# Four residual additions per column pair done by accumulating transfers instead of VectorE, in the gate stage of a one-core encoder block

## The chip, the cores and the metric

The kernel runs on one core of one Trainium2 chip. A core has TensorE for matrix products, VectorE and ScalarE for elementwise work, GpSimd (called POOL in the profile) and SyncE (SP), which here only issues transfers. The time is device microseconds of one execution; the runs before the change took 2024.7, 2026.38 and 2027.43 us, median 2026.38. An instruction of the profile carries the line of the kernel that made it, "L420" for line 420; a line can belong to a helper that many places call.

## The reference

One layer of a streaming encoder works on x, 256 rows of 4096 columns, all in f32. Attention and a convolution branch give y, which is projected and added to x. What the change touches comes after that:

```python
h = h + jnp.concatenate([y_a, y_c], axis=-1) @ w_out[i]
gate = jax.nn.sigmoid(rms_norm(h, ple_norm_g[i]) @ w_ple_gate[i] + b_ple_gate[i])
h = h + gate * (p[i] @ w_ple[i])
return rms_norm(h, final_g)
```

So the last stage needs the product of the normalised h with w_ple_gate (4096 x 4096), a bias per column, a sigmoid, a small product p @ w_ple (inner size 256), the gated residual addition, and the sum of squares of the new h per row for the final norm, whose weight is final_g.

## The kernel before, in words

**Products in two parts.** Each f32 matrix is split into a high part (cast to fp32r on ScalarE, L204) and a low part (subtracted on VectorE, L205); a product is the sum of three matmuls, high by high, low by high and high by low. All these matmuls into the large products come from line 420, those of the small embedding product from L237, those of weights kept back for the end of the last pair from L408.

**Column pairs.** The 4096 columns are eight blocks of 512, taken two at a time: four pairs, c0 = 0, 2, 4, 6. The 256 rows are two halves of 128, so a pair has four quarters (half h, block j), in the order (0,0), (1,0), (0,1), (1,1), and four PSUM banks that collect its product. The inner 4096 is cut into 16 units of 256 rows of weights. A plain unit is 24 matmuls. A unit marked * in an order such as `dense` uses a scheme of seven products instead of eight (21 matmuls); for it VectorE forms sums of weight tiles (L518, L519, L531, L532), and four more PSUM banks hold the helper sums P1, P5, P7 and P6. These four come from the same four banks (`ps_tmp`) into which the small product p @ w_ple goes. The order `dense` begins "1 0* 3 2*", so the helper banks are first needed in the second unit of a pair, unit 1 when counted from 0. Orders of the last stage hold eight * units, the order `final` of the last pair seven; its last three units are kept back as parts (`left`) and multiplied at the end quarter by quarter, with line-by-line order fixed by hand.

**Filler work.** Work that may run beside the products is put into a queue, `later`. After each unit `fill(4)` takes four entries from its front and traces them. The end of a pair puts work there that runs during the next pair's units: `gated_pair` (L1236) appends four products "embedding times gate" (which read, and so free, the `ps_tmp` banks) and then, quarter by quarter, the residual addition, the square sum and the weighting by final_g.

**What sets the order.** The program is traced in order, but a planner orders the instructions of each engine before the run. It gives a slot of a tile's buffers when one is free in its own reckoning, and it prefers what was traced first, yet fills an engine with later work whenever the earlier isn't ready by its reckoning. On the chip each engine then runs its list strictly in order and waits where it must. Only instructions under `pin` keep the written order. Weight tiles have five buffers (`wpool`), high parts and low parts three each, rows of bias and of final_g three (`row`). SP issues weight loads at L482 and the rows at L1071 (`broadcast_row`); POOL issues accumulating transfers, which in the stages before add one operand to a tile while they load it (L463, L495, L524). In the gate stage POOL issues none.

**The tail.** After the last pair come the kept-back products, both halves' norms and the stores, all pinned.

Of the kernel before, what the change touches and what calls it, by code (L numbers as in the profile page):

```python
# [13 lines left out]
ALU = mybir.AluOpType  # L14
# [3 lines left out]
NB = 512  # L18
# [7 lines left out]
def hybrid_block(  # L26
# [23 lines left out]
    nc = tc.nc  # L50
# [129 lines left out]
    later = deque()  # L180
# [62 lines left out]
    def product(w, col, lhs, kblocks, pool=None, tag="acc", fills=2):  # L243

        acc = [
            (pool or ps_acc).tile([P, NB], F32, tag=tag, name=f"acc{h}") for h in range(NH)
        ]
        for k0 in range(0, kblocks, KC):
            kc = min(KC, kblocks - k0)
            wh, wl = weight_parts(w, col, k0, kc)  # L250
            for k in range(kc):
                for h in range(NH):
                    accumulate(acc[h], h, lhs, k0 + k, wh, wl, k, kblocks)
            fill(fills)
        return acc
# [121 lines left out]
    def mixed_product(  # L377
# [93 lines left out]
        for n, (pair, seven, by_dma) in enumerate(order):  # L471
# [82 lines left out]
            if begins and on_begin:  # L554
                on_begin()
# [13 lines left out]
    tt, stt = nc.vector.tensor_tensor, nc.vector.scalar_tensor_tensor  # L569
    QUARTERS = ((0, 0), (1, 0), (0, 1), (1, 1))  # L570

    def helper_sums(helper, z):


        nc.scalar.copy(z[1][0], helper["P1"])
        tt(z[1][0], helper["P6"], z[1][0], ALU.add)
        tt(z[0][1], helper["P5"], z[1][0], ALU.add)
        tt(z[1][0], helper["P7"], z[1][0], ALU.add)
        tt(z[1][1], helper["P5"], z[1][0], ALU.add)

    def sum_tiles(*homes):

        homes = homes or (dict(tag="stage"),) * 2
        t = [spool.tile([P, NH, NB], F32, name="z", **kw) for kw in homes]
        return t, [[t[j][:, h] for j in range(2)] for h in range(NH)]
# [57 lines left out]
    def first_pairs(add):  # L643
# [62 lines left out]
        for n in range(1, n_x + 1):  # L706
# [26 lines left out]
    rows = [(conv_ln_g, KCW), (conv_ln_b, KCW), (b_dw, KCW), (attn_out_g, AW // P),  # L733
            (conv_out_g, KCW), (ple_norm_g, KD)]
# [332 lines left out]
    def broadcast_row(src, n0, n, **kw):  # L1067

        kw = kw or dict(tag="row", bufs=3)
        t = spool.tile([P, n], F32, name="row", **kw)  # L1070
        nc.sync.dma_start(  # L1071
            t, bass.AP(tensor=src.tensor, offset=src.offset + n0, ap=[[0, P], [1, n]])
        )
        return t
# [13 lines left out]
    for c0, order in zip(range(0, CW // NB, 2), point):  # L1088
        row = broadcast_row(b_pw, c0 * NB, 2 * NB, tag="stage")
        rows = [row[:, j * NB : (j + 1) * NB] for j in range(2)]  # L1090
# [106 lines left out]
    for c0 in range(0, D // NB, 2):  # L1197
        for j in range(2):
            hc = act.tile([P, NH, NB], F32, tag="act", name="hc")
            c = c0 + j  # L1200
# [19 lines left out]
        for h, j in QUARTERS:  # L1220
            hc = hs[c0 + j][:, h, :]
# [10 lines left out]
    ssq_f = cpool.tile([P, NH, n_f + 2], F32, name="ssq_f")  # L1232
    nc.vector.memset(ssq_f[:, :, :1], EPS)
    square_f = partial(square_sum, scale=D ** -0.5)

    def gated_pair(c0, order, ahead):  # L1236

        z, rows, fgs = [], [], []

        def on_begin():  # L1240
            rows.extend(broadcast_row(b_ple_gate, (c0 + j) * NB, NB) for j in range(2))

        def on_helpers(helper):
            z.extend(sum_tiles()[1])
            stt(z[0][0], helper["P1"], r_h[:, :1], rows[0], ALU.mult, ALU.add)
            helper_sums(helper, z)
            for h, j in QUARTERS[1:]:
                zz = z[h][j]
                stt(
                    zz, zz, r_h[:, h : h + 1], rows[j],  # L1250
                    ALU.mult, ALU.subtract if j else ALU.add,
                )
            fgs.extend(broadcast_row(final_g, (c0 + j) * NB, NB) for j in range(2))

        acc = mixed_product(
            w_ple_gate[0], c0 * NB, hT, hS, order, on_helpers, ahead=ahead, fills=(4,),
            on_begin=on_begin,
        )
        pacc = [
            product(w_ple[0], (c0 + j) * NB, pT, PLE // P, pool=ps_tmp, tag="tmp", fills=0)  # L1260
            for j in range(2)
        ]
        todo = []
        for h, j in QUARTERS:
            gt, hc = z[h][j], hs[c0 + j][:, h, :]
            stt(gt, acc[h][j], r_h[:, h : h + 1], gt, ALU.mult, ALU.subtract if j else ALU.add)
            nc.scalar.activation(gt, gt, AF.Sigmoid)
            later.append(partial(tt, gt, pacc[j][h], gt, ALU.mult))
            todo.append(partial(tt, hc, hc, gt, ALU.add))
            todo.append(partial(square_f, ssq_f[:, h, 1 + c0 + j : 2 + c0 + j], hc))  # L1270
            todo.append(partial(tt, hc, hc, fgs[j], ALU.mult))
        later.extend(todo)

    for c0 in range(0, n_f - 2, 2):
        gated_pair(c0, dense if c0 else late, None if c0 else h_ahead)


    c0 = n_f - 2
# [9 lines left out]
    rows, fgs = [], []  # L1288

    def on_begin():  # L1290
        rows.extend(broadcast_row(b_ple_gate, (c0 + j) * NB, NB) for j in range(2))

    def scaled(h, j):
        zz = z[h][j]
# [2 lines left out]
    def on_helpers(helper):  # L1297
# [3 lines left out]

    acc, add_left = mixed_product(
        w_ple_gate[0], c0 * NB, hT, hS, final, on_helpers, fills=(4,), on_begin=on_begin,
        left=[None] * 3 + [kept] * 3,
    )
# [73 lines left out]
    squares = []  # L1379
# [45 lines left out]
```

## Time and profile before

| | before |
|---|---|
| median of three runs | 2026.38 us |
| profiled execution, its own time | 2025.85 us |
| span of that execution in the trace | 2024.1 us |
| instructions | 26329 |
| granted TensorE clock | 0.998 |
| HBM read | 441.78 MB |

The time outside the span is 2025.85 - 2024.1 = 1.75 us. The gate stage is the last part of the span, from about 1690 us to the end. A busy share is an average over the whole span, and TensorE's includes the overlap of pipelined matmuls: a matmul of 128 x 512 is shown with 391 ns, while one starts about every 227 ns. Lost time of TensorE is therefore read from how many matmuls a stretch holds.

### The profile page before, as it was taken

Reading aid. Unit: us, or ns where it says so; the run is one execution under the profiler, and the core shown is the slowest. Engines: PE = TensorE matmul, PEld = TensorE weight load, DVE = VectorE, ACT = ScalarE, POOL = GpSimd, SP = SyncE. Lnnn points to the kernel's source line nnn. Section 1 sums busy time; section 2 is a strip of 40 time slices with the busy share of each in tenths; the row PEclk is TensorE's granted clock in tenths of the full one; section 3 lists DMA queues with packets and bytes.
Section 4 is the critical chain, followed back from the end, with each engine's and each line's share of the span. In section 5 each row is a group of like instructions: output and inputs, shape, how many; then the busy total and the mean of one; then the engine's idle time right before and its main releaser. Section 6 shows DMA issues by size and latency. Waiting matters only on the chain.

```text
span 2024.1 us, 26329 instructions
## 1 busy us (share of the span) xinstructions
PE 2006.7 (99%) x9043; PEld 1648.0 (81%) x9043; DVE 1926.9 (95%) x2771; ACT 1257.1 (62%) x1634; POOL 65.3 (3%) x71
## 2 busy tenths in 40 slices
PE   9999999999999999999999999999999999999997
PEld 7888888878888888788888888887888888888876
DVE  7999999899999999888999999999999999999998
ACT  7655555665666556776566676765766766656565
POOL 0000000000000000000000000000000000000000
PEclk9999999999999999999999999999999999999999
DMA  8788878679668877556677786876767766666765
GB/s 290 225 233 241 249 221 250 178 220 257 200 198 257 255 206 235 164 176 205 202 239 215 225 244 209 240 239 204 236 215 230 234 200 200 211 218 206 232 207 180
DMA packets 174193, 447.72 MB, mean 221 GB/s; under 512 B 14302, under 2 KB 17518, under 8 KB 174058
## 3 DMA queue, kind: packets, MB, share of 16 engines
q1 hardware_dynamic: 161952, 417.93, 63.8%
q0 software_dynamic: 11456, 27.27, 7.9%
q8 instruction: 71, 1.16, 0.2%
q10 hardware_dynamic: 650, 0.84, 0.1%
q14 instruction: 64, 0.52, 0.1%
HBM read 441.78 MB, written 4.19 MB: 220 GB/s over the span
## 4 chain that ended last, share of the span: by engine, by line
PE 89%; DVE 6%; issue 2%; DMA 1%; ACT 1%; POOLq 0%; POOL 0%; ACTq 0%; DVEq 0%; SPq 0%
PE acc L420 68%; PE acc_P L420 17%; DVE wl L205 2%; DMA wt<-in_w_in_dram 1%; PE tmp_ps L170 1%; DVE cv L787 1%; PE acc L237 1%; DVE ul L205 1%; PE tmp_ps L959 0%; PE tmp_ps L943 0%; PE tmp_ps L977 0%; ACT uh L204 0%; DVE cv L868 0%; ACT wh L204 0%; PE tmp_ps L982 0%
## 5 line engine op out<-in xcount | busy, mean ns | idle before, releaser
L420 PE MATMUL acc<-wh,big_t 128*128 128x512 f32 x4028 | 1240.3, 391 | 0.9 <-ACT big_t L156 0.4
L204 ACT CAST wh<-wt 128x1024 fp32r<-128x1024 f32 (+1 forms) x716 | 684.3, 965 | 493.8 <-PE acc L420 351.7
L420 PEld LDWEIGHTS acc<-wh,big_t 128*128 128x128 f32 x4028 | 753.3, 188 | 157.1 <-issue 1.3
L205 DVE TENSOR_TENSOR wl<-wt,wh 128x1024 fp32r<-128x1024 f32 (+1 forms) x716 | 788.8, 1113 | 33.0 <-ACT wh L204 27.5
L420 PE MATMUL acc<-wl,big_t 128*128 128x512 f32 x1958 | 756.4, 392 | 0.3 <-DVE wl L205 0.2
L420 PEld LDWEIGHTS acc<-wl,big_t 128*128 128x128 f32 x1958 | 367.2, 188 | 78.1 <-DVE wl L205 2.7
L204 ACT CAST uh<-ua 128x1024 fp32r<-128x1024 f32 x187 | 196.6, 1051 | 103.0 <-DVE ua L519 51.7
L205 DVE TENSOR_TENSOR ul<-ua,uh 128x1024 fp32r<-128x1024 f32 x187 | 228.1, 1220 | 6.9 <-ACT uh L204 4.2
L787 DVE SCALAR_TENSOR_TENSOR cv<-uT,dw,cv 128x255 f32<-128x255 f32 (+23 forms) x480 | 203.6, 463 | 1.1
L420 PE MATMUL acc_P<-uh,big_t 128*128 128x512 f32 x570 | 174.6, 391 | 0.1
L204 ACT CAST uh<-ub 128x1024 fp32r<-128x1024 f32 x99 | 104.2, 1053 | 47.9 <-DVE ub L532 39.2
L420 PEld LDWEIGHTS acc_P<-uh,big_t 128*128 128x128 f32 x570 | 106.0, 188 | 24.5 <-ACT uh L204 3.3
L205 DVE TENSOR_TENSOR ul<-ub,uh 128x1024 fp32r<-128x1024 f32 x99 | 120.8, 1220 | 0.8 <-ACT uh L204 0.5
L420 PE MATMUL acc_P<-ul,big_t 128*128 128x512 f32 x285 | 109.7, 392 | 0.2 <-DVE ul L205 0.2
L420 PE MATMUL acc<-uh,big_t 128*128 128x512 f32 x286 | 88.6, 390 | 0.0
L420 PE MATMUL acc_P<-wh,big_t 128*128 128x512 f32 x286 | 88.3, 389 | 0.0
L518 DVE TENSOR_TENSOR ua<-wt 128x512 f32<-128x512 f32 x112 | 76.9, 686 | 10.0 <-DMA wt<-in_w_in_dram 6.2
L519 DVE TENSOR_TENSOR ua<-wt 128x512 f32<-128x512 f32 x112 | 76.8, 686 | 2.7 <-DMA wt<-in_w_in_dram 1.7
L420 PE MATMUL acc_P<-uh,comb_t 128*128 128x512 f32 x228 | 70.3, 391 | 0.3 <-ACT uh L204 0.2
L532 DVE TENSOR_TENSOR ub<-ub,wt 128x512 f32<-128x512 f32 x99 | 68.1, 688 | 1.4
L531 DVE TENSOR_TENSOR ub<-ua,wt 128x512 f32<-128x512 f32 x99 | 67.8, 685 | 0.0
L420 PEld LDWEIGHTS acc_P<-ul,big_t 128*128 128x128 f32 x285 | 53.3, 188 | 13.9 <-DVE ul L205 3.0
(254 smaller groups left out, 1631.0 us busy)
## 6 DMA issues: line engine op xcount, KB each, us to landing
wt<-in_w_in_dram SPq DMA_DIRECT2D x416, 512.0 KB, 4.7
wt<-in_w_out_dram SPq DMA_DIRECT2D x128, 512.0 KB, 4.5
wt<-in_w_ple_gate_dram SPq DMA_DIRECT2D x128, 512.0 KB, 4.2
wt<-in_w_pw_dram SPq DMA_DIRECT2D x32, 512.0 KB, 4.9
ua<-in_w_in_dram SPq DMA_DIRECT2D x31, 512.0 KB, 4.3
ua<-in_w_in_dram POOLq DMA_DIRECT2D x31, 512.0 KB, 8.8
wt<-in_w_in_dram SPq DMA_DIRECT2D x31, 256.0 KB, 2.8
low<-in_w_in_dram POOLq DMA_DIRECT2D x12, 512.0 KB, 8.2
```

Source lines behind the costliest of these rows:

```text
L170: nc.tensor.transpose(pt[:, i * T + h * P : i * T + (h + 1) * P], src[:, h, b] if len(src.shape) == 4 else src[:, h, b * P : (b + 1) * P], ...
L204: nc.scalar.copy(wh[:, :kc, :], wt[:, :kc, :]),
L205: nc.vector.tensor_tensor(wl[:, :kc, :], wt[:, :kc, :], wh[:, :kc, :].bitcast(F32), ALU.subtract),
L237: nc.tensor.matmul(acc, a, b[:, k, :], start=kb == 0 and kind == 0, stop=kb == kblocks - 1 and kind == 2,)
L420: nc.tensor.matmul(banks[name], a, b, start=name not in begun, stop=final and ends[name] == n and kind == 2 and not (left and name in "P2 ...
L518: plus(ua[:, 0], w0[:, 0], w0[:, 1])
L519: plus(ua[:, 1], w0[:, 1], w1[:, 1])
L531: plus(ub[:, 0], ua[:, 0], w1[:, 1])
L532: plus(ub[:, 1], ub[:, 0], w1[:, 0])
L787: nc.vector.scalar_tensor_tensor(cv[:, i, PAD - k :], uT[:, i, : T + k - PAD], dw[:, b, k : k + 1], cv[:, i, PAD - k :], ALU.mult, ALU.add,)
```

## The change

In `gated_pair` the residual addition `hc + gt`, a VectorE instruction on 128 x 512 values, becomes a transfer issued by POOL that adds the tile `gt` onto `hc` in place. The queue `later` is refilled in another order: for each quarter the product, then its transfer (eight entries), then eight empty entries, then the four square sums, then the four weightings. With four entries per unit, the square sums are traced in unit 4 of the next pair and the weightings in unit 5. The products of the last two quarters are traced in unit 1 instead of unit 0. The two loads of a pair's bias rows, issued before in the first unit with helper sums, become two entries at the end of the same queue, in all four pairs. The last pair's own residual additions stay on VectorE.

The change's short name also speaks of seven products in a ninth pair and of three low parts by transfers in two groups; the diff has no line for that, and the kernel before has both already (the order `denser` has nine * units, and three marked "-").

```diff
+    def bias_row(rows, c):
+        rows.append(broadcast_row(b_ple_gate, c * NB, NB))
+
     def gated_pair(c0, order, ahead):
 
         z, rows, fgs = [], [], []
 
         def on_begin():
-            rows.extend(broadcast_row(b_ple_gate, (c0 + j) * NB, NB) for j in range(2))
+            later.extend(partial(bias_row, rows, c0 + j) for j in range(2))
...
-        todo = []
+        squares, weights = [], []
         for h, j in QUARTERS:
             gt, hc = z[h][j], hs[c0 + j][:, h, :]
             stt(gt, acc[h][j], r_h[:, h : h + 1], gt, ALU.mult, ALU.subtract if j else ALU.add)
             nc.scalar.activation(gt, gt, AF.Sigmoid)
             later.append(partial(tt, gt, pacc[j][h], gt, ALU.mult))
-            todo.append(partial(tt, hc, hc, gt, ALU.add))
-            todo.append(partial(square_f, ssq_f[:, h, 1 + c0 + j : 2 + c0 + j], hc))
-            todo.append(partial(tt, hc, hc, fgs[j], ALU.mult))
-        later.extend(todo)
+            later.append(partial(nc.gpsimd.dma_start, hc, gt, accum_op=ALU.add))
+            squares.append(partial(square_f, ssq_f[:, h, 1 + c0 + j : 2 + c0 + j], hc))
+            weights.append(partial(tt, hc, hc, fgs[j], ALU.mult))
+        later.extend([lambda: None] * 8 + squares + weights)
...
     def on_begin():
-        rows.extend(broadcast_row(b_ple_gate, (c0 + j) * NB, NB) for j in range(2))
+        later.extend(partial(bias_row, rows, c0 + j) for j in range(2))
```

## The prediction

> **What bounds it now.** I read the page first, then a table of four stretches of the last stage, then the chain of waits for the edges of its column pairs, and last the timelines of VectorE, ScalarE and TensorE around one edge. From the page:
>
> ```profile
> span 2024.1 us, 26329 instructions
> PE 2006.7 (99%) x9043; PEld 1648.0 (81%) x9043; DVE 1926.9 (95%) x2771; ACT 1257.1 (62%) x1634; POOL 65.3 (3%) x71
> PE 89%; DVE 6%; issue 2%; DMA 1%; ACT 1%; POOLq 0%; POOL 0%; ACTq 0%; DVEq 0%; SPq 0%
> ```
>
> TensorE is the bound, VectorE is nearly as full. Since a busy TensorE is not TensorE at its peak, I price its lost time in the part that the diff can touch: from the first matmuls behind pair 0 to the last of the final pair. The chain of waits, cut to three windows, gives the edges:
>
> ```profile
> 1740.13 5.44 PE acc L237 x24
> ...
> 1827.88 5.44 PE acc L237 x24
> ...
> 1915.73 5.44 PE acc L237 x24
> ```
>
> Twenty-four undisturbed matmuls take 5.44 us, so one takes 0.2267. The table by stretches (span, then busy time and count by engine, granted clock, DMA share, GB/s; the fourth and fifth rows are the L420 and L408 matmuls alone):
>
> ```profile
> 1745.57:1833.32 87.75, 87.70 (x386) 71.56 (x385) 87.02 (x106) 52.42 (x64) 0.00 (x0) 1.00 0.67 217
> 1833.32:1921.17 87.85, 87.85 (x385) 71.64 (x385) 86.98 (x107) 51.92 (x64) 0.00 (x0) 1.00 0.69 215
> 1921.17:1993.08 71.91, 71.73 (x309) 56.45 (x307) 70.82 (x87) 44.06 (x53) 0.00 (x0) 1.00 0.66 208
> ...
> 1921.17:1993.08 71.91, 67.88 (x291) 53.25 (x290) 1.00 0.66 208
> 1921.17:1993.08 71.91, 4.01 (x17) 3.19 (x17) 1.00 0.66 208
> ```
>
> By the code a middle pair has 8 units of 21 matmuls, 8 of 24 and 24 for the embedding: 384, or 87.04 us. It takes 87.75 and 87.85, so 0.71 and 0.81 are lost. In the final pair 291 + 17 = 308 matmuls are 69.81 us of 71.91: 2.10 lost. Together **3.6 us** is all that TensorE loses there. VectorE is idle for 0.73, 0.87 and 1.09 us of the same stretches and ScalarE for some 35 us of a pair: whatever is lost, VectorE is the engine that is late.
>
> **Removed: twelve additions.** Groups by line, last stage:
>
> ```profile
> L184 DVE TENSOR_TENSOR hc<-hc,row 128x512 f32<-128x512 f32 x12 | 8.2, 687 | 0.0
> L184 DVE TENSOR_TENSOR hc<-hc,z 128x512 f32<-128x512 f32 x12 | 8.1, 685 | 0.0
> ```
>
> The second group goes: 4 x 0.685 = 2.74 us of VectorE per pair boundary, three times, 8.2 us. It cannot bring 8.2. TensorE has only 0.71, 0.81 and 2.10 to win in the stretches behind the three boundaries, each less than 2.74. So the gain is between 0 and 3.6. It is 0 if the lost slivers come from hand-overs between ScalarE and VectorE and not from the backlog; it is 3.6 if the backlog is all. Since the high and low parts have three buffers each, VectorE can't keep 2.74 us of lead for 70 us; I take somewhat under half, 1.5.
>
> **Added: twelve transfers on POOL.** Each is 128x512 f32, 256 KB, read twice and written once, all inside SBUF. The trace has no such transfer; the nearest rows are the accumulating loads, and plain ones of that size. Two lines of POOL issues (L495's landing, then L524's issue and landing) and the page's list of issues:
>
> ```profile
> DMA to landing us min/median/max: 5.8/7.0/9.3
> ...
> L524 POOL DMA_DIRECT2D low<-in_w_out_dram x6: 859/860/872, 1445.6 to 1615.2; - x6
> DMA to landing us min/median/max: 8.0/8.7/10.0
> ...
> low<-in_w_out_dram POOLq DMA_DIRECT2D x9, 512.0 KB, 8.4
> ...
> row<-in_b_ple_gate_dram SPq DMA_DIRECT2D x8, 256.0 KB, 4.7
> ...
> out_dram<-hc SPq DMA_DIRECT2D x12, 256.0 KB, 2.4
> ```
>
> Issue: 0.86 us each on POOL, which has 0.00 busy in all three stretches, so it costs nothing; without that cover it would be 12 x 0.86 = 10.3 us. Landing: not under the 2.4 of a plain store from SBUF, not over the 8.7 of an accumulating load of twice the bytes; I take 5.5, between the plain 4.7 and the accumulating 7.0. The Trainium skill's page "DMA: Bandwidth & Descriptors", section "Anatomy of one DMA — SWDGE (gpsimd) path", fits 2.0 us plus bytes over 436e3 per microsecond, an estimate of 2.6 us here; the trace does not agree, for the same fit gives 3.2 us for the 512 KB rows that took 7.0 and 8.7. By the fit the square's wait below would vanish and the sum would be 0.3 us better.
>
> Do they crowd out weights? Three transfers of twice the size fall into one stretch of the output projection:
>
> ```profile
> 1438.83:1460.00 21.17, 21.17 (x93) 17.38 (x93) 20.47 (x27) 15.51 (x18) 2.58 (x3) 1.00 0.97 262
> ```
>
> The DMA share is 0.97 there against 0.67, and 93 matmuls in 21.17 us are 0.2276 each, the full pace within a count. Four transfers of half the size bring less. Cost 0; at worst the 0.2 us that these 93 lie above 0.2267, per boundary.
>
> **Moved: two products.** Transfers now stand between the products, so of the first four entries taken in unit 0 two are transfers, and the products of quarters (0,1) and (1,1) slip into unit 1. They empty two PSUM banks that unit 1's helper sums P7 and P6 need. At the second boundary VectorE, ScalarE and TensorE ran so:
>
> ```profile
> 1832.68 1.88 DVE L184 TENSOR_TENSOR z<-acc,z 128x512 f32<-128x512 f32 x3
> ...
> 1836.28 0.69 DVE L531 TENSOR_TENSOR ub<-ua,wt 128x512 f32<-128x512 f32 x1
> 1836.94 1.23 DVE L205 TENSOR_TENSOR wl<-wt,wh 128x1024 fp32r<-128x1024 f32 x1
> ...
> 1839.82 1.29 DVE L184 TENSOR_TENSOR hc<-hc,z 128x512 f32<-128x512 f32 x2
> 1841.02 1.22 DVE L205 TENSOR_TENSOR wl<-wt,wh 128x1024 fp32r<-128x1024 f32 x1
> 1842.16 1.22 DVE L205 TENSOR_TENSOR ul<-ub,uh 128x1024 fp32r<-128x1024 f32 x1
> ```
> ```profile
> 1835.85 1.06 ACT L204 CAST wh<-wt 128x1024 fp32r<-128x1024 f32 x1 [2.05 <-PE acc L420]
> ...
> 1838.61 2.00 ACT L204 CAST wh<-wt 128x1024 fp32r<-128x1024 f32 x2 [0.76 <-ACT uh L204]
> 1840.52 1.05 ACT L204 CAST uh<-ub 128x1024 fp32r<-128x1024 f32 x1
> 1841.46 0.63 ACT L610 ACTIVATE junk<-hc 128x512 bf16<-128x512 f32 x1
> ```
> ```profile
> 1838.60 0.62 PE L420 MATMUL acc_P<-wh,big_t 128*128 128x512 f32 x2
> ...
> 1839.96 0.62 PE L420 MATMUL acc_P<-uh,big_t 128*128 128x512 f32 x2
> ...
> 1842.00 0.62 PE L420 MATMUL acc_P<-uh,big_t 128*128 128x512 f32 x2
> ```
>
> The slots that unit 1 gives to filler work are those where two additions ran at 1839.82. With two products fewer ahead of them they come 1.2 us sooner (three took 1.88), near 1838.6, or in the gap that opens before the low part at 1836.94, which waits for a cast that TensorE releases. The banks are then free at about 1839.3 and 1839.9; P7 starts at 1839.96 and P6 at 1842.0. It fits, barely: cost 0, at worst the rival below.
>
> **Moved: squares, weightings, bias rows.** Four squares (ScalarE) and four weightings (VectorE, 0.687 us) keep their number and go to units 4 and 5; eight empty entries make the distance. The two bias-row loads are issued behind the weightings instead of in unit 1. Their 0.33 us on SP's queue are the same; they are read some 13 units later, so a landing of 4.7 us is hidden, and their wait for a free row no longer stands ahead of weights by order of the program. Cost 0. But the planner fills idle engines with any ready work. Behind the first pair of the output projection, ScalarE:
>
> ```profile
> 1403.28 0.63 ACT L610 ACTIVATE junk<-hc 128x512 bf16<-128x512 f32 x1 [1.31 <-DVE hc L1222]
> ...
> 1406.55 1.03 ACT L204 CAST wh<-wt 128x1024 fp32r<-128x1024 f32 x1
> 1407.61 1.05 ACT L204 CAST uh<-ua 128x1024 fp32r<-128x1024 f32 x1
> ```
>
> Two of the four squares in this group belong, in program order, behind unit 1's casts of 1406.55 and 1407.61, and ran before them; ScalarE even held 1.31 us for the first. So a square may be put ahead of its transfer's real landing, with unit 1's and 2's casts queued behind it and VectorE's low parts behind these. If kept in unit 4 it has some 15 us, and nothing is late. I charge 0.1 us per boundary, 0.3 in all.
>
> **Sum.** -1.5 + 0.3 = -1.2 us. The profiled execution took 2025.85, its span 2024.1 and 1.75 outside; it becomes 2024.65. The median of the runs shown, 2026.38, lies 0.53 above it, so I forecast **2025.2**.
>
> **Rivals.** *All of the lost time returns*: 2026.38 - 3.6 = 2022.8. For it: VectorE is over 98% busy wherever TensorE loses, and 2.74 exceeds every loss. Against: three buffers cap its lead. *Nothing moves*, 2026.4: the freed time becomes idle VectorE, or a different planned order eats it.
>
> *Squares run ahead*, on the slower side. The transfer of quarter (1,0) goes out after its product, about 1834; at the upper landing, 8.7 us, it is there at 1842.7. If its square sits in ScalarE's hole before 1838.61, the casts behind it wait 4.1 us; 0.76 of that is idle now, and the low parts lie 1.1 us ahead of their matmuls (1841.02 + 1.22 against the end of unit 1's 21, 1838.60 + 4.76). TensorE loses the other 2.2 us; the second two transfers land within the delay. Three boundaries: 6.6 - 1.2 = +5.4, 2031.8. It decides once a transfer lands over 2 us later than the planner believes. For it: the squares at 1403.28. Against: the 35 us of slack of ScalarE and a landing nearer 5.5. That would also be the change not doing what it says, three units.
>
> *Banks late*: if the two products come only behind the low part that ends at 1843.4, P7 waits from 1839.96 to about 1842.8, 2.9 us a boundary, 8.6 - 1.2 = +7.4, 2033.8.
>
> **Chances.** Forecast 0.42, nothing 0.26, all 0.13, squares 0.13, banks 0.06. A measurement of this kernel can tell about 0.2%, 4.05 us, from no change. The first three lie within it, yet spread over it a little on either side: faster 0.08, same 0.74, slower 0.18. The range goes from just under the whole gain, 2022.4, to the price of the squares, 2031.9; the likeliest case alone would be 2023.6 to 2026.2.
>
> **What would show it.** Right: no L184 additions of hc on VectorE before the tail, twelve POOL issues near 0.86 us, VectorE's busy time down by about 2.7 in each stretch while the two middle pairs stay above 87.04. Wrong: ScalarE waiting on a transfer in a square, TensorE waiting at P7 or P6 for a product, SP held in a bias row, or a landing above 8.7 us. A time below 2022.3 would mean that the 3.6 us is no bound.

## The result

The changed kernel takes 2049.24 us (median of four runs, 2046.09 to 2052.6) against 2026.41 for the kernel before (median of four, too). The ratio is 1.0114, 95% interval 1.0099 to 1.0129: 22.8 us slower. The forecast was 2025.2 us and the range ended at 2031.9.

The page of the profile after, span and engines, and then from the list of transfers by issue (size of one, median time from issue to landing) two rows:

```profile
span 2047.0 us, 26349 instructions
PE 2009.9 (98%) x9043; PEld 1648.4 (81%) x9043; DVE 1922.0 (94%) x2759; ACT 1258.1 (61%) x1634; POOL 75.8 (4%) x83
```
```profile
wt<-in_w_ple_gate_dram SPq DMA_DIRECT2D x128, 512.0 KB, 4.2
...
hc<-z POOLq DMA_DIRECT2D x12, 256.0 KB, 6.0
```

The twelve additions have left VectorE (2771 to 2759 instructions) and twelve transfers are on POOL (71 to 83). TensorE has the same 9043 matmuls. The three stretches that the prediction priced, with the same edges in the program (386, 385 and 309 matmuls in view), in the table by stretches:

```profile
1747.13:1841.70 94.57, 88.74 (x386) 71.42 (x384) 85.61 (x103) 52.48 (x64) 3.73 (x5) 1.00 0.70 211
1841.70:1937.90 96.20, 89.05 (x385) 71.39 (x384) 85.34 (x102) 52.53 (x63) 3.34 (x5) 1.00 0.67 208
1937.90:2015.38 77.48, 71.98 (x309) 56.80 (x308) 70.21 (x84) 44.96 (x54) 2.83 (x4) 1.00 0.71 214
```

They took 87.75, 87.85 and 71.91 us before: 6.82 + 8.35 + 5.57 = 20.7 of the 22.9 us by which the span grew. TensorE's granted clock is 1.00 in all three stretches of this execution, and the DMA share hardly moved. VectorE, nearly full before, is idle for 9 to 11 us of each middle pair. Both fell behind something else. The list of who waited for whom names it (total, times, longest; over the whole span):

```profile
ACT junk L610 <- DMA hc<-z: 31.2, 12, 5.4
...
PE acc_P L420 <- DVE ul L205: 7.1, 9, 1.7
PE acc_P L420 <- DVE z L184: 6.9, 3, 2.7
```

Every one of the twelve squares held ScalarE until its transfer had landed. The same list for TensorE alone, from 1747.13 to 2015.38, has four lines, and for the same stretches of the kernel before it is empty:

```profile
PE acc_P L420 <- DVE z L184: 6.9, 3, 2.7
PE acc_P L420 <- DVE ul L205: 6.6, 6, 1.7
PE acc_P L420 <- ACT uh L204: 2.7, 6, 0.7
PE acc_P L420 <- ACT wh L204: 2.1, 1, 2.1
```

So 18.3 of the 20.7 us are TensorE standing still for a product (first line), a low part (second) or a cast (the last two), all of them made on ScalarE or VectorE. The first boundary in the timelines of ScalarE, VectorE, POOL and TensorE (start, length, in brackets the idle time before and what ended it):

```profile
1750.76 0.63 ACT L610 ACTIVATE junk<-hc 128x512 bf16<-128x512 f32 x1 [2.04 <-DMA hc<-z]
...
1753.17 0.63 ACT L610 ACTIVATE junk<-hc 128x512 bf16<-128x512 f32 x1 [1.70 <-DMA hc<-z]
...
1753.81 1.03 ACT L204 CAST wh<-wt 128x1024 fp32r<-128x1024 f32 x1
...
1761.46 0.63 ACT L610 ACTIVATE junk<-hc 128x512 bf16<-128x512 f32 x1 [3.78 <-DMA hc<-z]
...
1765.58 0.63 ACT L610 ACTIVATE junk<-hc 128x512 bf16<-128x512 f32 x1 [2.89 <-DMA hc<-z]
```
```profile
1754.87 1.22 DVE L205 TENSOR_TENSOR wl<-wt,wh 128x1024 fp32r<-128x1024 f32 x1 [3.47 <-ACT wh L204]
1756.01 0.68 DVE L184 TENSOR_TENSOR z<-acc,z 128x512 f32<-128x512 f32 x1
...
1757.74 0.68 DVE L184 TENSOR_TENSOR z<-acc,z 128x512 f32<-128x512 f32 x1
```
```profile
1757.33 0.87 POOL L184 DMA_DIRECT2D hc<-z  x1 [8.96 <-issue]
1759.08 0.86 POOL L184 DMA_DIRECT2D hc<-z  x1 [0.87 <-PE acc L420]
```
```profile
1756.75 0.73 PE L420 MATMUL acc_P<-uh,big_t 128*128 128x512 f32 x2 [2.66 <-DVE z L184]
```

Read them as one chain. Two squares sit on ScalarE before the cast at 1753.81 and wait 2.04 and 1.70 us. The low part on VectorE waits 3.47 us for that cast. Behind the low part, in VectorE's list, stands the product of quarter (0,1); it runs at 1756.01, and TensorE stands 2.66 us at the helper sum whose bank that product frees. Because the product is late, its transfer is issued only at 1757.33 and the fourth at 1759.08, so the next two squares, again ahead of casts, wait 3.78 and 2.89 us more. The delay of the first two squares lengthens that of the last two; the first experiment shows what is left of it when no product is late.

### The profile page after: what moved, and what is told of

It is laid out like the page before. It is cut to its first block, busy times and chain, and to the rows that moved or that the text cites. A ratio compares the mean times of both kernels' runs of the same rounds, so it can differ in the third digit from the quotient of the medians.

```text
span 2047.0 us, 26349 instructions
## 1 busy us (share of the span) xinstructions
PE 2009.9 (98%) x9043; PEld 1648.4 (81%) x9043; DVE 1922.0 (94%) x2759; ACT 1258.1 (61%) x1634; POOL 75.8 (4%) x83
## 5 line engine op out<-in xcount | busy, mean ns | idle before, releaser
L420 PEld LDWEIGHTS acc_P<-ul,big_t 128*128 128x128 f32 x285 | 53.3, 188 | 22.3 <-DVE ul L205 11.3
```

What stands on the lines that cost most here:

```text
L420: nc.tensor.matmul(banks[name], a, b, start=name not in begun, stop=final and ends[name] == n and kind == 2 and not (left and name in "P2 ...
```

## The experiments

Each is set against the kernel before, run on the same chip; its medians in the three groups of runs were 2025.71, 2026.53 and 2025.33 us. Three theories were put to the test: squares run ahead of their transfers' landing on ScalarE; the products moved to unit 1 free their banks too late by themselves; the transfers crowd the DMA engines. Two side issues are the bias rows and the distance of three units.

**Products first.** All four products are traced ahead of the four transfers, in unit 0 as before the change.

```diff
-            later.append(partial(nc.gpsimd.dma_start, hc, gt, accum_op=ALU.add))
+            adds.append(partial(nc.gpsimd.dma_start, hc, gt, accum_op=ALU.add))
...
-        later.extend([lambda: None] * 8 + squares + weights)
+        later.extend(adds + [lambda: None] * 8 + squares + weights)
```

> All four products stand ahead of the four transfers again, so they are traced in unit 0 and free the helper banks as before; squares are left where the planner puts them. 'Squares run ahead' (ScalarE sat 31.2 us in squares waiting for transfers, with casts queued behind): only the 6.9 us of TensorE at P7 go, about 2041 us, and ScalarE still waits over 20 us in squares. 'Banks late' (the products traced in unit 1 are the cause): back to about 2027 us. 'Transfers crowd the DMA engines': no change, 2049 us.

2043.98 us, ratio 1.0085 (1.007 to 1.01). The waits list of this kernel:

```profile
ACT junk L610 <- DMA hc<-z: 19.0, 8, 5.2
...
PE acc_P L420 <- ACT uh L204: 12.6, 6, 5.9
```

TensorE's wait for a product has gone from the list, and with the last two transfers out earlier only eight squares wait. In its place TensorE waits for casts themselves, 12.6 us over the whole span against 1.5 in the kernel before. Against the kernel before on the same chip 18.3 of the 22.8 us stay, so late banks are not the root; time and waits missed the expected 2041 and "over 20" by a little. At the first boundary the last two squares still wait 2.00 and 2.12 us, though no product is late there: their own places in ScalarE's list are too early as well.

Part of these 18.3 us is a slower clock. In this trace TensorE's granted clock fell to 0.50 around its longest stop, which ended at 1763.04, and stayed there for some us of work (stretch and length, then busy time and count by engine, granted clock, DMA share, GB/s):

```profile
1760.00:1762.00 2.00, 0.00 (x0) 0.00 (x0) 0.88 (x1) 2.00 (x5) 0.00 (x0) 0.50 0.26 107
1764.00:1766.00 2.00, 2.00 (x6) 1.56 (x5) 2.00 (x4) 0.00 (x0) 0.00 (x0) 0.50 0.95 332
```

It fell after the stops of 1.97 and 2.26 us at the other two boundaries too. Counted at 0.2267 us per matmul, the three slow stretches cost an estimated 1.6, 1.7 and 1.7 us. The profiled execution of the changed kernel, with a stop of 2.66 us, shows no such fall; its mean clock is 0.998, but the other three timed runs have 0.993 to 0.996, where the kernel before has 0.997 or 0.998. When a stop is followed by the slower clock stays open.

**Squares held.** The products stay in unit 1; each square is queued on ScalarE behind the last cast made when the filler work of its unit is traced (`recent` holds that cast, and `queued_behind` adds an edge of order alone, no wait).

```diff
+    def held_square(dst, src):
+        with queued_behind(recent[:1]):
+            square_f(dst, src)
...
-            squares.append(partial(square_f, ssq_f[:, h, 1 + c0 + j : 2 + c0 + j], hc))
+            squares.append(partial(held_square, ssq_f[:, h, 1 + c0 + j : 2 + c0 + j], hc))
```

> Each square is queued on ScalarE behind the last cast of unit 4, where it was traced; the products stay in unit 1. 'Squares run ahead': ScalarE's waits on transfers fall from 31.2 us to under 2, VectorE gets its casts in time and the late product with them, 2024 to 2029 us. 'Banks late' as a cause of its own: the 6.9 us at P7 stay, about 2033 us. 'Transfers crowd the DMA engines': 2045 us or more.

2025.31 us, ratio 0.9995 (0.9986 to 1.0004): the whole loss is gone with these edges. No square waits for a transfer any more. ScalarE at the first boundary of this kernel:

```profile
1752.22 2.00 ACT L204 CAST wh<-wt 128x1024 fp32r<-128x1024 f32 x2 [0.30 <-PE acc L420]
...
1762.42 2.00 ACT L204 CAST wh<-wt 128x1024 fp32r<-128x1024 f32 x2 [0.72 <-ACT uh L204]
1764.33 0.62 ACT L610 ACTIVATE junk<-hc 128x512 bf16<-128x512 f32 x1
```

In the changed kernel the first square ran at 1750.76; here it runs at 1764.33, in unit 4, where the program had put it. The products are still in unit 1 and 12 transfers still run, so neither is a cause of its own.

**Both repairs.** Products first and squares held.

> Products first and squares held behind unit 4's last cast. 'Squares run ahead': 2023 to 2027 us, within 2 us of the variant with held squares alone, and the middle pairs take under 88 us each. 'Banks late': 2023 to 2027 us and clearly below the variant with held squares alone. 'Transfers crowd the DMA engines': over 2035 us, with TensorE waiting for weights.

2023.63 us, ratio 0.999 (0.9981 to 1.0). The same kernel was run once more in more rounds:

> Products first and squares held, once more, in more rounds: whether the repaired change is a gain. 'VectorE's freed 8.2 us are worth something': 0.5 to 3 us below the kernel before, the interval under 1. 'Worth nothing': the interval holds 1 in its middle.

2024.49 us, ratio 0.9994 (0.9985 to 1.0003). Both medians are lower than the kernel before by 0.8 to 2.1 us; neither interval excludes 1. The middle pairs of the second profile:

```profile
1745.84:1833.29 87.45, 87.45 (x385) 71.82 (x384) 85.51 (x102) 52.68 (x64) 3.62 (x5) 1.00 0.73 229
1833.29:1920.78 87.49, 87.49 (x385) 71.76 (x384) 85.21 (x103) 52.69 (x63) 3.41 (x4) 1.00 0.73 228
```

They need 87.45 and 87.49 us where the kernel before took 87.75 and 87.85 and 384 matmuls at 0.2267 us are 87.04: some of the slivers came back. The profile of the first run gives 87.42 and 87.50 us.

**Bias rows alone.** The kernel before, with the two row loads put into the queue's end and nothing else.

```diff
-            rows.extend(broadcast_row(b_ple_gate, (c0 + j) * NB, NB) for j in range(2))
+            later.extend(partial(bias_row, rows, c0 + j) for j in range(2))
```

> The kernel before with one part of the change alone: the bias-row loads become the last two entries of the queue. All theories that blame squares, products or transfers: 2026.4 us, no difference that can be measured. 'Rows late on SP': part of the 23 us, 2030 us or more, with SP held in a row load ahead of weights.

2025.47 us, ratio 1.0001 (0.9991 to 1.001): nothing.

**More empty entries.** The changed kernel with 24 empty entries for 8.

```diff
-        later.extend([lambda: None] * 8 + squares + weights)
+        later.extend([lambda: None] * 24 + squares + weights)
```

> The changed kernel with 24 empty entries instead of 8, so squares and weightings are traced four units later still (units 8 and 9). 'Squares run ahead': the planner puts squares on ScalarE as soon as it reckons the transfer done, whatever unit they are traced in, so ScalarE still waits about 31 us and the time stays within 4 us of the changed kernel's 2049. 'Too short a distance' (three units don't cover the landing): the waits vanish and the time is about 2026.

2048.95 us, ratio 1.0109 (1.0096 to 1.0123), and in the waits list

```profile
ACT junk L610 <- DMA hc<-z: 29.5, 12, 4.2
```

Distance in the trace order did nothing, because the squares did not go where they were traced. The eight empty entries of the change were no protection either. How early the planner reckons a transfer landed is in no record, so whether a better estimate of it would have done as well as the edges stays open.

**Additions on VectorE in the changed order.** The transfers are replaced by the additions; the queue's order is that of the changed kernel.

```diff
-            later.append(partial(nc.gpsimd.dma_start, hc, gt, accum_op=ALU.add))
+            later.append(partial(tt, hc, hc, gt, ALU.add))
```

> The changed kernel with its queue order kept, but each of the twelve transfers replaced by the addition on VectorE. 'Squares run ahead of a landing': nothing to land, so ScalarE's squares wait under 1 us each and the time is 2025 to 2029 us. 'The order itself' (products in unit 1, squares late): 2040 us or more although no transfer is left.

2026.68 us, ratio 1.0003 (0.9994 to 1.0012). The squares run ahead here too, the first of them at 1744.93, but what they wait for is an instruction of VectorE, and the waits are short:

```profile
ACT junk L610 <- DVE hc L184: 3.6, 5, 1.5
```

Five waits, the longest 1.5 us and so over the expected 1, cost nothing that shows. In these runs running ahead cost time only where the thing waited for was a landing.

**Held, without distance.** Both repairs and no empty entries, so the squares are held in unit 2.

```diff
-        later.extend(adds + [lambda: None] * 8 + squares + weights)
+        later.extend(adds + squares + weights)
```

> Products first, squares held behind the last cast of the unit in which they are traced, and no empty entries: squares in unit 2 instead of unit 4. A landing of about 6 us after issues that end in unit 1 still fits before unit 2's last cast or misses it by a little. 'Only the planner's place matters': 2023 to 2027 us, as with the empty entries. 'Held squares need the distance too': 2030 us or more, with ScalarE waiting over 10 us on transfers.

2027.84 us, ratio 1.0004 (0.9995 to 1.0013). Three squares still wait:

```profile
ACT junk L610 <- DMA hc<-z: 4.2, 3, 1.9
```

The median lies 0.84 us above the expected band, yet the interval cannot be told from no change. Two units are on the edge of the landing, four are clear of it.

**Additions held.** Both repairs, with additions on VectorE for the transfers: it differs from the kernel with both repairs in the transfers alone.

> The variant with products first and held squares, but with the additions on VectorE. It differs from that variant in the twelve transfers alone. 'VectorE's freed 8.2 us are worth something': 1 to 3 us slower than with transfers, about 2025 to 2027 us. 'Freed VectorE time is worth nothing': equal to it within 1 us.

2025.81 us, ratio 0.9999 (0.999 to 1.0008), against 0.999 and 0.9994 with the transfers. The middle pairs of its profile:

```profile
1744.78:1832.98 88.20, 88.20 (x385) 71.50 (x384) 87.36 (x106) 52.51 (x64) 0.00 (x0) 1.00 0.68 217
1832.98:1921.21 88.23, 87.95 (x385) 71.62 (x384) 87.40 (x107) 52.32 (x63) 0.00 (x0) 1.00 0.66 214
```

They are 0.75 and 0.74 us longer than with the transfers (87.45, 87.49), with VectorE 1.85 and 2.19 us busier. By these two profiles, one of each variant, the transfers gain about 0.7 us a pair (against the kernel before, whose order differs, 0.30 and 0.36); by the times the gain lies within the intervals. Held squares without transfers are no faster than the kernel before, so the edges only take the loss away.

**Two of four held.** The changed kernel with only the last two squares of each boundary held.

```diff
-            squares.append(partial(square_f, ssq_f[:, h, 1 + c0 + j : 2 + c0 + j], hc))
+            squares.append(partial(held_square if j else square_f, ssq_f[:, h, 1 + c0 + j : 2 + c0 + j], hc))
```

> The changed kernel with only the last two squares of each boundary held behind unit 4's last cast; the first two stay where the planner puts them, ahead of casts. 'Squares run ahead': the loss scales with the waits that are left. In the changed kernel the first boundary's waits were 2.04 and 1.70 us for the first two squares and 3.78 and 2.89 for the last two, so 10 to 14 us of ScalarE's 31 stay and the time lies between, 2032 to 2040 us. If one pair of squares alone carried the loss, it would be 2026 or 2048 us.

2036.69 us, ratio 1.0058 (1.0044 to 1.0071), inside the band expected. Its waits list:

```profile
ACT junk L610 <- DMA hc<-z: 11.3, 6, 3.2
...
PE acc_P L420 <- DVE z L184: 5.9, 3, 2.2
```

The wait for the products' banks is nearly what it was (6.9), so it hangs on the first two squares. Set beside the medians' losses, the waits of ScalarE on transfers go 0, 11.3, 19.0, 29.5, 31.2 us with -0.4, 11.4, 18.3, 22.4, 22.8 us lost (squares held, two held, products first, 24 empty entries, the change). The losses hold the slower clock as well: it shows 0.50 somewhere in the traces of two held, products first and 24 empty entries.

**Both repairs, and far.** Held squares with 24 empty entries.

> The same with 24 empty entries instead of 8, so that held squares and weightings fall in units 8 and 9. 'VectorE's freed time pays where its work is thinned': 1 us or more below the variant with 8, since the filler work is spread over more units. 'The lead is capped by three buffers': equal within 1 us.

2023.23 us, ratio 0.9989 (0.998 to 0.9998): 2.1 us below the kernel before, the only one of eleven variants whose interval lies under 1, and by a hair; one such interval in eleven is weak evidence. Its middle pairs:

```profile
1745.19:1832.26 87.07, 87.07 (x385) 72.03 (x384) 84.73 (x102) 52.98 (x64) 3.31 (x5) 1.00 0.73 229
1832.26:1919.48 87.22, 87.22 (x385) 72.00 (x384) 85.49 (x104) 52.72 (x63) 3.79 (x5) 1.00 0.73 230
```

87.07 and 87.22 us stand against the floor of 87.04. That it beats the variant with 8 empty entries by 1.3 us in the median is within the spread of either (2021.2 to 2026.46 and 2022.4 to 2027.34), so whether thinner filler work pays stays open.

## Why the prediction was wrong

**The bound and the removed additions held.** TensorE could win at most 3.6 us here, and no median lies further below the kernel before than 2.1. With both repairs and empty entries the two middle pairs lose 0.46 us or less in every profile where the kernel before lost 0.71 and 0.81. The three medians with both repairs and empty entries lie 0.8 to 2.1 us lower; 1.5 agrees with that, but two of their three intervals reach 1, so it is not confirmed.

**The step that failed is "Moved: squares".** It charged 0.1 us per boundary on the ground that a square "if kept in unit 4" has 15 us. It was not kept there. The row at 1403.28, quoted just before, showed this planner putting squares ahead of casts, and the text then still took the kept case as likeliest. The three stretches behind the boundaries lost 20.7 us more than before in the trace, and the runs put them there: held squares bring all of it back, and 24 empty entries bring nothing.

**The rival "squares run ahead" was the right mechanism at a fraction of its size and with a chance of only 0.13.** It priced one wait of 4.1 us per boundary, 2.2 of it lost, and said that "the second two transfers land within the delay". They don't: a delayed cast delays the low part, this the product, and this the issue of the third and fourth transfer. Four waits of 2.04, 1.70, 3.78 and 2.89 us, 10.4 us at the first boundary, took the place of one. The price of a single wait was close: with the products first, one square at the second boundary waits 4.96 us and one at the third 5.24, and TensorE stands 1.97 and 2.26 us at the late cast behind them. What the price lacked was the number of waits, the chain between them and, in some executions, the slower clock behind a stop. The landing itself was well placed (5.5 taken, 6.0 measured); lateness relative to the place in the list decides, not its length.

**"Against: the 35 us of slack of ScalarE" was a wrong reading.** In the three stretches of the kernel before ScalarE is idle for 99.1 us; 57.2 of them end with a matmul that frees the buffer of its next cast, and 20.0 with a sum of weight tiles on VectorE. Such time is spread over the whole pair, and only the piece right in front of a late cast can take up its delay (the 0.76 us in the rival's own sum). Beyond it there was the lead of 1.1 us, computed a few sentences before. VectorE went idle for 3.47 us at once.

**"Moved: two products" was priced at 0, "banks late" at 2.9 us a boundary and a chance of 0.06.** TensorE waited there 2.7 us at most, 6.9 in all, but as a consequence: with held squares and the products still in unit 1 the whole kernel is at 0.9995. The two rivals were told as separate; in the changed kernel the second was a consequence of the first.

**Crowding and the rows** were rightly at nothing. The DMA share in the changed stretches is 0.67 to 0.71, twelve transfers with held squares lose nothing, and the rows alone measure 1.0001. The fit in the Trainium skill's page "DMA: Bandwidth & Descriptors", section "Anatomy of one DMA — SWDGE (gpsimd) path", an estimate of 2.6 us for these transfers, does not agree with the 6.0 of this trace.

The range ended at the price of the squares, and even both rivals' prices added, 6.6 and 8.6 us less the 1.2 of the sum, give 14.0 of the 22.8 us: they were single waits without what a wait does to the next.

## What to carry to other kernels

When an in-order engine takes over a wait for a transfer, ask where the planner puts the waiting instruction, not where the code does, and pin it behind the work that must not wait; empty entries in a queue are no pin where engines have idle time. Idle time of an engine that waits for buffers is not slack: the slack is how far its results lie ahead of their reader. When several waits hang on one another, follow the first delay through to the issue of the next transfer before pricing them as parallel.

## What was not expected of the hardware

An accumulating transfer of 256 KB from SBUF into SBUF takes 6.0 us from issue to landing, longer than the 4.2 of a plain 512 KB weight load from HBM in the same stage, which SP issues on its own queue (no run tells the queue from the accumulation):

```profile
DMA to landing us min/median/max: 3.9/6.0/8.3
```

This row is that of the transfers into hc in the changed kernel. In the repaired kernel four of them per boundary go with a DMA share of 0.73 in the middle pairs, against 0.67 and 0.69 before, without slowing TensorE.

A short stop of TensorE can cost more than its length: after some stops of 2 to 6 us its granted clock was 0.50 for some us in three of the traces (products first, 24 empty entries, two held), and it stayed at 1.00 after stops of 1.88 to 2.66 us in that of the changed kernel.
